# Shared accumulation banks in the up projection, both last down-projection pairs by seven products, and a denser weave in attention

## The chip, the cores and the metric

The kernel runs on one core of one Trainium2 chip. The metric is the device time of the execution in microseconds. A run's profile gives one execution: the time of each instruction on TensorE (PE), VectorE (DVE), ScalarE (ACT), GpSimd (POOL) and the DMA queues, which SyncE (SP), POOL and ACT issue.

## The reference

A decoder trunk of two layers over 256 tokens of width 2048, in fp32. Layer 0 has differential attention, layer 1 latent attention; each layer then attends to 256 memory tokens and ends in the MLP on which most of the change bears:

```
def sq_relu_mlp(h, wup, wdown):
    return jnp.square(jax.nn.relu(h @ wup)) @ wdown
...
        x = x + sq_relu_mlp(rms_norm(x, mlp_norm[i]), mlp_wup[i], mlp_wdown[i])
    return rms_norm(x, final_norm)
```

`wup` is 2048 x 8192, `wdown` 8192 x 2048. In layer 0, `x + o @ wo` closes the attention, with `wo` 2048 x 2048.

## The kernel before

**Precision.** A product of fp32 matrices is three matmuls: weight and activation are each split into a rounded half (hi) and a rest (lo), and hi x hi, hi x lo and lo x hi are summed in a PSUM bank. ScalarE makes a weight's hi (L211), VectorE its lo (L212), each in two pieces of 128x1024; four such pieces are kept, so a split is at most two items ahead of TensorE. Weights arrive in 1 MB tiles of 128x2048 (seven of them, the pool `wraw`).

**Items.** `fill` emits an item's load and split four items ahead of its matmuls. A plain *unit* is one weight tile against both halves of the tokens (t = 0, 1): 24 matmuls of 512 columns. A *product* is one weight tile against one half: 12 matmuls.

**Seven products.** A block of the MLP takes 1024 of the 8192 hidden columns, as two chunks of 512. Blocks 1 to 7 of the up projection (class `Seven`) compute the 2 x 2 blocks (two token halves, two weight columns) by seven products p1 to p7 instead of eight, each in two steps x = 0, 1, so 14 items where the plain way has 8 units. Sums of activations (forms s1 to s4) are made once, sums of weights per block: two by VectorE (L837, `add` in `job`), one by an accumulating DMA on POOL's queue (L829). Each product has its own PSUM bank; ScalarE copies p1 and p5 out (L905), VectorE adds and subtracts the others (L899), and `out` then applies ReLU and square (L1421, L1422), transposes on TensorE and splits the hidden block.

The down projection adds each block's part onto x in four column chunks c = 0 to 3: a chunk of a block has two units, `Chunk` joins the chunks of neighbouring blocks in one open pair of banks, and VectorE adds the closed sum to x (L515). Of the last block (7), columns 2 and 3 go by seven products (class `Final`, items Fp1 to Fp7), whose banks are added onto x by L1027; columns 0 and 1 are plain. `Final` shares banks already: p6 and p7 go onto p1's, p3 onto p5's. Its weight sums come from two accumulating DMAs (L949) and two additions of VectorE (L952).

**Order.** TensorE's order is written out. `mlp_line` merges the list `rest` (up units of block 0, down units) with the list `seven` so that VectorE's work, estimated by `vector`, and TensorE's, `tensor`, stay in step (`lead`); `late` holds back a down unit whose hidden block isn't ready. The merged list is the *line*. Before the change it ends with three down units (`after`) and then the *end*: 4 plain units and 7 products of `Final`. ScalarE's and VectorE's order is made by the framework's scheduler from the order of emission and estimated times. Transposes and the work behind them are side tasks: `pump`, called after every half item, emits those that an estimated clock calls due.

**Attention of layer 0.** The last two row groups of `wo` are added plainly (`project_group`). The first two go as two pairs (class `Pair`, columns 0-1 and 2-3) of seven products, one woven behind each of the 12 units of the last q, k, v projection and of the first two units of the next `project_group`. A pair's weight sums are four accumulating DMAs on POOL's queue (`onto`, L949). Meanwhile the last head group's softmax runs (L576 to L728), whose `a` (L728) TensorE then transposes (L168).

**Queues.** SP issues all weight loads in order, each waiting for a free tile; POOL issues the accumulating DMAs in order, each waiting for the split that last read its target and for the load before it.

Of the kernel before, what the change touches and what calls it, by code (L numbers as in the profile page):

```python
# [25 lines left out]
MLP_BLOCKS = 8  # L26
SEVEN = (1, 2, 3, 4, 5, 6, 7)
EVS = 7

# [18 lines left out]
def trunk(ctx, tc, x, xT, xT0, mem, memT, positions, gcols, gfinal, lam_vecs, consts, W, out):  # L48
# [214 lines left out]
    def matmul_chunk(acts, width=CH, turns=False, by_k=False):  # L263
# [11 lines left out]
        for u in range(n - 2 if turns else n):  # L275
            if weave:
                weave[0].step()
# [11 lines left out]
            if weave:  # L289
                weave.pop(0).emit()  # L290
# [500 lines left out]
    def plan_mlp(l):  # L791
        plan.extend(j for line in mlp_lines[l] for item in line for j in item.jobs)
# [21 lines left out]
    class Seven:  # L814
# [65 lines left out]
        def products(self, a, u, copied, out):  # L880
# [17 lines left out]
            def add(o, p, q, op=ALU.add):  # L898
                nc.vector.tensor_tensor(o, p, q, op)  # L899

            c = copied
            if p in ("p1", "p5", "p6", "p3"):
                c[p] = work.tile([P, CH], F32, tag="ev", name=nm(p), bufs=EVS)
            if p in ("p1", "p5"):
                nc.scalar.copy(c[p], o)  # L905
            elif p == "p6":
                add(c[p], o, c["p1"])
            elif p == "p3":
                add(c[p], o, c["p5"])
                add(c[p], c[p], c["p6"], ALU.subtract)  # L910
                out(0, 1, c[p], c[p])
            elif p == "p2":
                add(c["p1"], o, c["p1"])
# [9 lines left out]
    class Final:  # L923
# [3 lines left out]
        ORDER = "p1 p2 p5 p6 p3 p7 p4".split()  # L927

        def __init__(self, l):
            self.l, self.b = l, MLP_BLOCKS - 1  # L930
            self.cols = (2, 3)
# [3 lines left out]
            self.forms = {}  # L935

        def source(self, key):
            return W[f"mlp_wdown{self.l}"][8 * self.b + 2 * (1 + key % 10) + key // 10 - 1]

        def fetch(self, key):  # L940
            self.raw[key] = raw_tile()
            load(self.raw[key], self.source(key))

        def home(self, key):
            self.raw[key] = f32(unit()).rearrange("p a k t -> p (a k t)")
            return self.raw[key]

        def onto(self, o, key):
            tc.keep_in_program_order(nc.gpsimd.dma_start(self.raw[o], self.source(key), accum_op=ALU.add))  # L949

        def sum(self, o, a, b):
            nc.vector.tensor_tensor(self.home(o), self.raw[a], self.raw[b], ALU.add)  # L952

        def early(self):
            return [
                lambda hid: (
                    self.sums([k for c in range(2) for k in hid[self.b, c].tasks]),
                    self.fetch(11), load(self.home("t1"), self.source(11)),
                ),
                lambda hid: (self.onto("t1", 12), self.fetch(22), self.fetch(21)),  # L960
                lambda hid: (self.sum("t2", "t1", 22), self.sum("t4", "t2", 21)),
                lambda hid: self.fetch(12),
                lambda hid: self.onto(12, 22),
            ]

        def job(self, p):
            source = {"p1": 11, "p2": 21, "p3": 22, "p4": "t4", "p5": "t1", "p6": "t2", "p7": 12}[p]
            return lambda: halves_of(self.raw[source])

        def items(self):  # L970
            return [Item(self, p, [self.job(p)]) for p in self.ORDER]
# [27 lines left out]
        def products(self, inputs, p, nxt):  # L999
            where = Seven.A[p]  # L1000
            if p in ("p1", "p2", "p4"):
                t, c = where
                need(inputs[c].tasks)
# [17 lines left out]
            for t, j, op in {  # L1021
                "p1": ((0, 0, ALU.add),), "p5": ((1, 1, ALU.add),), "p6": ((0, 1, ALU.subtract),), "p3": ((0, 1, ALU.add),),
                "p7": ((1, 1, ALU.subtract), (1, 0, ALU.add)), "p2": ((0, 0, ALU.add),), "p4": ((1, 0, ALU.add),),
            }[p]:
                xc = xs[t][:, self.cols[j] * CH : (self.cols[j] + 1) * CH]
# [4 lines left out]
            done = {"p2": (2, 0), "p3": (3, 0), "p7": (3, 1), "p4": (2, 1)}  # L1030
            if nxt and p in done:
                nxt(*done[p], o)

    class Pair(Final):

        ORDER = "p1 p2 p5 p3 p6 p7 p4".split()
        FETCH = {"p1": ((11, 11), ("t", 12)), "p2": ((21, 21),), "p3": ((22, 22),)}
        STEP = {"p1": ("t", 11), "p5": ("t", 22), "p3": (22, 12), "p6": ("t", 21)}  # L1040
        SPLIT = {"p1": 11, "p2": 21, "p5": "t", "p3": 22, "p6": "t", "p7": 22, "p4": "t"}

        def __init__(self, name, first, cols, forms):
            self.name, self.first, self.cols, self.forms = name, first, cols, forms
            self.raw = {}
            self.banks = {}
            self.parts = {}
            self.steps = []
            self.splits = []

        def source(self, key):
            return W[self.name][4 * self.cols[key % 10 - 1] + self.first + key // 10 - 1]

        def part(self, t, c):
            if not self.parts:
                store = f32(unit()).rearrange("p a k (h t) -> p a (k h) t", t=P)
                self.parts = {(i, j): store[:, i, 4 * j : 4 * j + 4] for i in range(NT) for j in range(2)}
            return self.parts[t, c]

        def job(self, p):  # L1060
            def run():
                for key, at in self.FETCH.get(p, ()):
                    self.raw[key] = raw_tile()
                    load(self.raw[key], self.source(at))
                before = {"p5": ["p1"], "p6": ["p1", "p5"], "p7": ["p3"], "p4": ["p1", "p5", "p6"]}.get(p, [])
                assert all(i in self.steps for i in before)
                self.splits.append(p)
                return halves_of(self.raw[self.SPLIT[p]])

            return run  # L1070

        def items(self, inputs):
            return [Woven(self, p, inputs) for p in self.ORDER]

    class Woven:
# [3 lines left out]
        def step(self):  # L1079
            if self.p in self.of.STEP:  # L1080
                after = {"p5": "p5", "p3": "p3", "p6": "p6"}.get(self.p)
                assert after is None or after in self.of.splits
# [733 lines left out]
```

## Time and profile before

| what | value |
| --- | --- |
| runs shown, median | 2209.9 us (2209.76 to 2210.2, 3 runs) |
| the profiled execution | 2209.08 us |
| its span, first to last instruction | 2207.3 us |
| TensorE busy | 2191.9 us, 10511 matmuls |
| VectorE busy | 1814.2 us, 2025 instructions |
| ScalarE busy | 1388.1 us, 1855 instructions |
| granted TensorE clock, mean | 0.998 |
| DMA, mean | 213 GB/s |

The profiled execution is 1.8 us longer than its span, the time around the first and last instruction. A matmul's end is modelled, and matmuls overlap: one of 512 columns is shown as 0.39 us long, while the next starts about 0.227 us after it. In rows of instructions come start and length in us, engine, line, operation and what is written from what; brackets give idle time before it and who ended it. Tiles `pr` are banks of products, `mm` of plain units.

### The profile page before, as it was taken

What the parts mean: (1) busy time and instruction counts of PE and PEld (TensorE: products, weight loads), DVE (VectorE), ACT (ScalarE), POOL (GpSimd) and SP (SyncE); (2) the same over time, 40 slices, a digit from 0 to 9 for tenths busy, and PEclk for the clock granted to TensorE, in tenths of its full rate; (3) what the DMA queues carried; (4) which work ended last, traced back from release to release, by engine and by line L of the source; (5) the groups of instructions that cost most, each with busy time, mean ns of one, the idle gap of its engine ahead of it and who ended that gap; (6) DMA issues with size and microseconds to landing.
All of it is one profiled execution on the core that took longest, in us unless ns stands there. A gap on an engine that the chain in (4) does not pass through costs nothing.

```text
span 2207.3 us, 27663 instructions
## 1 busy us (share of the span) xinstructions
PE 2191.9 (99%) x10511; PEld 1838.4 (83%) x10511; DVE 1814.2 (82%) x2025; ACT 1388.1 (63%) x1855; POOL 147.6 (7%) x230
## 2 busy tenths in 40 slices
PE   9999999999999999999999999999999999999998
PEld 7888888888888888888889988888888888888886
DVE  6665878789889888889886878778988998898888
ACT  7555656666666666666665755656766666666665
POOL 1112210000000000000000411000000000000001
PEclk9999999999999999999999999999999999999999
DMA  9447796436766765865865344634767667677693
GB/s 384 156 155 250 221 268 252 153 124 203 266 204 207 263 203 217 254 214 210 273 213 191 133 155 155 246 134 153 225 232 228 209 249 224 199 258 221 203 297 105
DMA packets 71702, 469.43 MB, mean 213 GB/s; under 512 B 8208, under 2 KB 8592, under 8 KB 17808
## 3 DMA queue, kind: packets, MB, share of 16 engines
q1 hardware_dynamic: 65520, 425.19, 53.5%
q0 software_dynamic: 5760, 41.95, 10.3%
q8 instruction: 82, 1.34, 0.2%
q10 hardware_dynamic: 288, 0.52, 0.1%
q14 instruction: 52, 0.43, 0.1%
HBM read 465.53 MB, written 2.10 MB: 212 GB/s over the span
## 4 chain that ended last, share of the span: by engine, by line
PE 91%; DVE 5%; issue 1%; ACT 1%; DMA 1%; POOL 0%; SPq 0%; DVEq 0%; POOLq 0%; ACTq 0%
PE mm L164 61%; PE pr L164 25%; PE ax L164 2%; DVE wlo L212 2%; PE ax L168 2%; PE mm L168 1%; DVE raw L837 1%; ACT whi L211 1%; DVE unit L459 0%; DVE raw L487 0%; DMA raw<-in_mlp_wup_dram 0%; POOL rs L401 0%; DMA raw<-in_xT_dram 0%; DVE raw L470 0%; DVE x L515 0%
## 5 line engine op out<-in xcount | busy, mean ns | idle before, releaser
L211 ACT CAST whi<-raw 128x1024 fp32r<-128x1024 f32 (+2 forms) x974 | 1012.3, 1041 | 681.4 <-PE mm L164 520.1
L212 DVE TENSOR_TENSOR wlo<-raw,whi 128x1024 fp32r<-128x1024 f32 (+2 forms) x974 | 1161.3, 1210 | 287.7 <-ACT whi L211 272.0
L164 PE MATMUL mm<-whi,unit 128*128 128x512 f32 (+3 forms) x4160 | 1320.7, 389 | 0.6 <-ACT unit L389 0.6
L164 PEld LDWEIGHTS mm<-whi,unit 128*128 128x128 f32 x4160 | 778.0, 188 | 151.5 <-ACT unit L389 2.0
L164 PE MATMUL mm<-wlo,unit 128*128 128x512 f32 (+3 forms) x2080 | 802.8, 386 | 0.9 <-DVE wlo L212 0.8
L164 PE MATMUL pr<-whi,unit 128*128 128x512 f32 x1792 | 579.9, 392 | 0.0
L164 PEld LDWEIGHTS mm<-wlo,unit 128*128 128x128 f32 x2080 | 391.7, 188 | 74.0 <-DVE wlo L212 3.1
L164 PEld LDWEIGHTS pr<-whi,unit 128*128 128x128 f32 x1792 | 336.8, 188 | 69.2
L164 PE MATMUL pr<-wlo,unit 128*128 128x512 f32 x896 | 349.7, 390 | 0.6 <-DVE wlo L212 0.6
L837 DVE TENSOR_TENSOR raw<-raw,raw 128x2048 f32<-128x2048 f32 x84 | 192.3, 2289 | 28.7 <-DMA raw<-in_mlp_wup_dram 28.3
L164 PEld LDWEIGHTS pr<-wlo,unit 128*128 128x128 f32 x896 | 168.5, 188 | 36.0 <-DVE wlo L212 1.8
L829 POOL DMA_DIRECT2D raw<-in_mlp_wup_dram x28 | 24.6, 877 | 1094.8 <-DVE wlo L212 1094.8
L515 DVE TENSOR_TENSOR x<-x,mm 128x512 f32<-128x512 f32 x128 | 84.9, 682 | 3.6 <-PE mm L164 3.4
L401 POOL TENSOR_TENSOR rs<-rs,mhalf 128x1 f32<-128x1 f32 (+1 forms) x26 | 27.5, 1063 | 535.1 <-DVE rs L400 535.1
L356 ACT CAST unit<-ax 128x512 fp32r<-128x512 f32 x68 | 39.4, 582 | 25.7 <-PE ax L168 25.7
L899 DVE TENSOR_TENSOR p<-pr,p 128x512 f32<-128x512 f32 x70 | 47.9, 685 | 2.7 <-PE pr L164 2.7
L357 DVE TENSOR_TENSOR unit<-ax,unit 128x512 fp32r<-128x512 f32 x68 | 46.5, 686 | 1.5 <-ACT unit L356 1.1
L164 PE MATMUL mm<-unit,whi 128*128 128x256 f32 x256 | 47.1, 285 | 0.1
L168 PE MATMUL ax<-identr,p 128*128 128x128 f32 x304 | 46.2, 272 | 0.5 <-ACT unit L1650 0.5
L168 PEld LDWEIGHTS ax<-identr,p 128*128 128x128 f32 x304 | 37.6, 139 | 10.8 <-ACT unit L1650 0.9
L1421 ACT ACTIVATE p<-p,r 128x512 f32<-128x512 f32 x56 | 40.3, 720 | 9.6 <-DVE p L899 9.5
L164 PEld LDWEIGHTS mm<-unit,whi 128*128 128x128 f32 x256 | 40.0, 192 | 0.4 <-DVE unit L357 0.3
(185 smaller groups left out, 1147.0 us busy)
## 6 DMA issues: line engine op xcount, KB each, us to landing
raw<-in_mlp_wup_dram SPq DMA_DIRECT2D x128, 1024.0 KB, 4.9
raw<-in_mlp_wdown_dram SPq DMA_DIRECT2D x128, 1024.0 KB, 5.1
raw<-in_da_wqkv_dram SPq DMA_DIRECT2D x45, 1024.0 KB, 7.3
raw<-in_mlp_wup_dram POOLq DMA_DIRECT2D x28, 1024.0 KB, 8.2
raw<-in_da_wo_dram SPq DMA_DIRECT2D x16, 1024.0 KB, 6.8
raw<-in_ca_wkv_dram SPq DMA_DIRECT2D x16, 1024.0 KB, 5.0
raw<-in_mla_wo_dram SPq DMA_DIRECT2D x16, 1024.0 KB, 5.0
raw<-in_da_wo_dram POOLq DMA_DIRECT2D x8, 1024.0 KB, 10.6
```

The lines of the kernel that those rows point to most:

```text
L164: return nc.tensor.matmul(o, stationary, moving, start=start, stop=stop, skip_group_check=onto)
L168: nc.tensor.transpose(o, src, ident)
L211: nc.scalar.copy(hi, r)
L212: nc.vector.tensor_tensor(lo, r, f32(hi), ALU.subtract)
L356: nc.scalar.copy(hi, src)
L357: nc.vector.tensor_tensor(dst[:, 1, :n, t * P : (t + 1) * P], src, f32(hi), ALU.subtract)
L401: nc.gpsimd.tensor_tensor(r[:, :n], r[:, :n], mhalf.broadcast_to([P, n]), ALU.pow)
L515: nc.vector.tensor_tensor(xc, xc, ps, ALU.add)
L829: tc.keep_in_program_order(nc.gpsimd.dma_start(onto, src, accum_op=ALU.add))
L837: nc.vector.tensor_tensor(o, o, q, ALU.add)
L899: nc.vector.tensor_tensor(o, p, q, op)
L1421: nc.scalar.activation(r, src, AF.Relu, scale=rstd[t])
```

## The change

Three parts. **(1) Up products:** in `Seven`, p6, p7 and p4 accumulate onto the bank of p1 and p3 onto that of p5, so sums form in PSUM. ScalarE copies p1, p5 and p6 out; VectorE is left with one subtraction for p3, one addition for p2, one subtraction for p7; p4 goes from its bank straight into the ReLU. A rule `apart` keeps p4 from following its block's p7 directly while `rest` has an item. **(2) Down projection:** `Final` is gone. Both pairs of the last block are `Pair`s, A for columns 0-1 and B for 2-3, sharing activation sums; their weight sums are four accumulating DMAs each. Block 6's eight units and two of block 5 move behind the line and are interleaved with the 14 products in the order `CLOSING` (u is a unit). Steps, each a DMA on POOL's queue, are issued at the items given by `put`. **(3) Attention:** the 14 woven products go into the 12 units by `WEAVE`, up to two behind one unit; none is left for `project_group`.

```diff
+LAST = MLP_BLOCKS - 1
+WEAVE = "A1", "A2", "A5", "A3", "A6 B1", "A7 B2", "A4", "B5", "B3", "B6", "B7", "B4"
+CLOSING = "u A1 u A2 u B1 u A5 B2 u B5 A6 u A3 u B6 u B3 u A7 u A4 B7 B4"
...
         for u in range(n - 2 if turns else n):
-            if weave:
-                weave[0].step()
+            for item in weave[0] if weave else ():
+                item.step()
...
-            if weave:
-                weave.pop(0).emit()
+            for item in weave.pop(0) if weave else ():
+                item.emit()
...
-            if x == 0:
+            on = {"p6": "p1", "p7": "p1", "p4": "p1", "p3": "p5"}.get(p, p)
+            if x == 0 and on == p:
                 self.banks[p] = bank("pr")
-            o = self.banks[p]
+            o = self.banks[on]
...
-                    mmul(o, form[:, 0, kk], wh, kk == 0, False)
-                    mmul(o, form[:, 0, kk], wl, False, False)
-                    mmul(o, form[:, 1, kk], wh, False, kk == 7)
+                    mmul(o, form[:, 0, kk], wh, kk == 0 and on == p, False, on != p)
+                    mmul(o, form[:, 0, kk], wl, False, False, on != p)
+                    mmul(o, form[:, 1, kk], wh, False, kk == 7, on != p)
...
-            if p in ("p1", "p5"):
+            if p in ("p1", "p5", "p6"):
                 nc.scalar.copy(c[p], o)
-            elif p == "p6":
-                add(c[p], o, c["p1"])
             elif p == "p3":
-                add(c[p], o, c["p5"])
-                add(c[p], c[p], c["p6"], ALU.subtract)
-                out(0, 1, c[p], c[p])
+                nc.vector.tensor_tensor(c["p6"], o, c["p6"], ALU.subtract)
+                out(0, 1, c["p6"], c["p6"])
...
             elif p == "p7":
-                add(c["p6"], o, c["p6"])
-                add(c["p5"], c["p5"], c["p6"], ALU.subtract)
+                nc.vector.tensor_tensor(c["p5"], c["p5"], o, ALU.subtract)
                 out(1, 1, c["p5"], c["p5"])
             else:
-                add(c["p6"], o, c["p6"])
-                out(1, 0, c["p6"], c["p6"])
+                out(1, 0, o, c["p4"])
...
+    class Pair:
+        FETCH = {"p1": (11, "t"), "p2": (21,), "p3": (22,)}
+        STEP = {"p1": ("t", 11), "p5": ("t", 22), "p3": (22, 12), "p6": ("t", 21)}
+        SPLIT = {"p1": 11, "p2": 21, "p5": "t", "p3": 22, "p6": "t", "p7": 22, "p4": "t"}
...
+        def step(self, p):
+            o, key = self.STEP[p]
+            assert p == "p1" or p in self.splits
             tc.keep_in_program_order(nc.gpsimd.dma_start(self.raw[o], self.source(key), accum_op=ALU.add))
+            self.steps.append(p)
...
-            chunks += [Chunk(l, "down", groups[i], c, close=False) for c in pairs[1]]
+            chunks += [Chunk(l, "down", groups[i], c, close=False) for c in pairs[1] if i < LAST - 2 or c == 2]
...
-        rest = up(0, 1) + [i for b in range(MLP_BLOCKS - 1) for i in down(b)]
+        rest = up(0, 1) + [i for b in range(LAST - 1) for i in down(b)]
...
-        rest, after = rest[:-3], rest[-3:]
...
-            late = rest and of.kind == "down" and any(usable.get(h, math.inf) > now for h in of.halves)
-            take_seven = seven and (not rest or late or lead <= 0)
+            late = rest and of.kind == "down" and usable.get(of.halves[rest[0].u], math.inf) > now
+            apart = seven and seven[0].u == ("p4", 0) and line[-1].of is seven[0].of
+            take_seven = seven and (not rest or late or (lead <= 0 and not apart))
...
-        end = down(len(groups) - 1)
-        for item, step in zip(after + end, end[-1].of.early()):
-            item.early = step
-        return line + after, end
+        plain = [
+            i
+            for c in range(4)
+            for i in Chunk(l, "down", both(LAST - 2, *both(LAST - 1)) if c == 3 else both(LAST - 1), c, open=c != 2).items()
+        ]
+        forms = {}
+        pairs = {k: Pair(f"mlp_wdown{l}", 8 * LAST, 2, c, forms) for k, c in (("A", (0, 1)), ("B", (2, 3)))}
+        end = []
+        at = {}
+        for word in CLOSING.split():
+            at[word] = len(end)
+            if word == "u":
+                end.append(plain.pop(0))
+            else:
+                of, p = pairs[word[0]], "p" + word[1]
+                end.append(Item(of, p, [of.job(p)]))
...
+        put(0, lambda hid: pairs["A"].sums([k for c in range(2) for k in hid[LAST, c].tasks]))
+        for k, of in pairs.items():
+            put(max(0, at[k + "1"] - 3), lambda hid, of=of: of.fetch("t", of.home()))
+            put(at[k + "1"] - 1, lambda hid, of=of: of.step("p1"))
+        for p in ("p5", "p6", "p3"):
+            for k, of in pairs.items():
+                put(at[k + p[1]] - 3, lambda hid, of=of, p=p: of.step(p))
+        for i, todo in steps.items():
+            end[i].early = lambda hid, todo=todo: [do(hid) for do in todo]
+        return line, end, pairs["A"]
```

More of the change, by code (lines that the diff above doesn't have):

```diff
@@ L934, in __init__ @@
             self.parts = {}
-            self.forms = {}
+            self.steps = []
+            self.splits = []
         def source(self, key):
[L938 to L946, printed above, removed]
@@ L966, in job, with fetch @@
-        def job(self, p):
[L967 to L971, printed above, removed]
+            at = 12 if key == "t" else key
+            return W[self.name][self.first + self.stride * self.cols[at % 10 - 1] + at // 10 - 1]
+        def fetch(self, key, home=None):
+            if key not in self.raw:
+                self.raw[key] = raw_tile() if home is None else home
+                load(self.raw[key], self.source(key))
@@ new lines, in home, with run @@
+        def home(self):
+            return f32(unit()).rearrange("p a k t -> p (a k t)")
+        def step(self, p):
+            o, key = self.STEP[p]
+            assert p == "p1" or p in self.splits
+            tc.keep_in_program_order(nc.gpsimd.dma_start(self.raw[o], self.source(key), accum_op=ALU.add))
+            self.steps.append(p)
+        def job(self, p):
+            def run():
+                for key in self.FETCH.get(p, ()):
+                    self.fetch(key)
+                before = {"p5": ["p1"], "p6": ["p1", "p5"], "p7": ["p3"], "p4": ["p1", "p5", "p6"]}.get(p, [])
+                assert all(i in self.steps for i in before)
+                self.splits.append(p)
+                return halves_of(self.raw[self.SPLIT[p]])
+            return run
@@ L973, in keep, with part @@
+        def part(self, t, c):
+            if not self.parts:
+                store = f32(unit()).rearrange("p a k (h t) -> p a (k h) t", t=P)
+                self.parts = {(i, j): store[:, i, 4 * j : 4 * j + 4] for i in range(NT) for j in range(2)}
+            return self.parts[t, c]
         def keep(self, t, c, src):
@@ L1029, in products @@
                     added.append(summed)
[L1030 to L1073, printed above, removed]
+                if landed:
+                    landed(c, t, o, p in ("p2", "p3", "p7", "p4"))
     class Woven:
@@ L1165, in trunk @@
+    plan += [("da_wo", 4 * c + 2, CH) for c in range(4)]
     plan_k("ca_wkv0", 4)
@@ L1459, in run @@
                     continue
[L1460 to L1461 removed]
+                if isinstance(of, Pair):
+                    of.products([hid[LAST, c] for c in range(2)], item.u, landed)
                     continue
@@ L1473, in run @@
                 if item.u == n - 1 and of.close:
-                    finish_chunk(of, sums.pop((of.kind, of.c)), nxt)
-        line, end = mlp_lines[l]
+                    finish_chunk(of, sums.pop((of.kind, of.c)), landed)
+        line, end, pair = mlp_lines[l]
         limit = free_banks[0] - 1
```

117 lines of the change are left out of this document (50 added, 67 removed).

## The prediction

> **What bounds the kernel now.** I read the page first, then TensorE's waits, then the chain of waits.
>
> ```profile
> span 2207.3 us, 27663 instructions
> ...
> PE 2191.9 (99%) x10511; PEld 1838.4 (83%) x10511; DVE 1814.2 (82%) x2025; ACT 1388.1 (63%) x1855; POOL 147.6 (7%) x230
> ...
> PE 91%; DVE 5%; issue 1%; ACT 1%; DMA 1%; POOL 0%; SPq 0%; DVEq 0%; POOLq 0%; ACTq 0%
> ```
>
> The first line is the span, the second each engine's busy share, the third the shares of the chain that ended last. TensorE is busy for all but 2207.3 - 2191.9 = 15.4 us, most of it before the first and after the last matmul. VectorE, at 82%, is second.
>
> ```profile
> PE ax L168 <- DVE a L728: 1.2, 1, 1.2
> PE mm L164 <- DVE wlo L212: 0.8, 2, 0.4
> PE pr L168 <- DVE x L1027: 0.6, 1, 0.6
> PE pr L164 <- DVE wlo L212: 0.6, 2, 0.3
> ```
>
> These are the waits of TensorE that the change can reach (total us, times, longest). They come to 3.2 us. So the kernel can gain by fewer matmuls and hardly by anything else, and every wait that the change puts in front of TensorE is paid in full.
>
> ```profile
> 537.72 5.44 PE mm L164 x24
> 543.16 5.44 PE pr L164 x24
> ```
>
> Start, length, count, from the chain: 24 matmuls of 512 columns take 5.44 us, plain (mm) or of seven products (pr): 0.2267 us each. A plain unit (24 matmuls) is 5.44 us, a product (12) 2.72 us.
>
> **a. The second pair by seven products.** Of the last block's down projection, columns 2 and 3 go by seven products already. Columns 0 and 1 take 4 plain units, 4 x 24 = 96 matmuls a layer. They become 7 x 12 = 84. Two layers: 24 matmuls less, 24 x 0.2267 = **-5.4 us**. That block 6's units and one chunk of block 5 move behind the line changes no count. Attention keeps all its products.
>
> **b. The shared banks.** p6, p7 and p4 now add onto the bank of p1, p3 onto that of p5. A product's first matmul must wait until the bank's last reader is through. I worked out the order of items by the planner's rule. p1 to p6, p5 to p3 and p6 to p7 always have at least a product and a unit between them, 8.2 us, and p7 to p4 has one unit, 5.44 us, since `apart` holds p4 back. At one place it can't: `rest` is used up when block 7's last product comes, and each layer's line ends "unit, p7, p4, p4". There p4 waits for VectorE's subtraction (now `c5 - o`) from that bank. What it will take is seen at the same product of before:
>
> ```profile
> 2127.75 0.39 PE L164 MATMUL pr<-whi,unit 128*128 128x512 f32 x1
> 2127.98 0.39 PE L164 MATMUL mm<-whi,unit 128*128 128x512 f32 x1
> ```
>
> ```profile
> 2126.55 2.58 DVE L212 TENSOR_TENSOR wlo<-raw,whi 128x1024 fp32r<-128x1024 f32 x2
> 2129.05 0.69 DVE L899 TENSOR_TENSOR p<-pr,p 128x512 f32<-128x512 f32 x1
> ```
>
> The product's last matmul starts at 2127.75, and the next item, which today needs nothing, at 2127.98. VectorE is splitting weights until 2129.1 and reads the bank until 2129.74. TensorE starts about 0.05 us after such an end (below). So p4 starts at about 2129.79: 1.8 us late, twice: **+3.6 us**. From below: with VectorE free, the read would start at the matmul's end, 2127.75 + 0.39 = 2128.14, and p4 at 2128.88: 0.9 us, +1.8 in all. From above, the slowest kind of such read in the line:
>
> ```profile
> 1710.95 5.46 PE mm L164 x24
> ```
>
> ```profile
> 1714.32 0.68 DVE L899 TENSOR_TENSOR p<-pr,p 128x512 f32<-128x512 f32 x1
> ```
>
> The unit behind p7 starts at 1710.95 and the read ends at 1715.00: 4.1 us with the restart, +8.2 in all. I take 1.8, from the very place; no next block's sums crowd VectorE there. At the other p7s the same 4.1 us stay under the unit's 5.44 us, so they cost nothing, and would cost the excess if the read came 1.4 us later.
>
> The new sharing also moves work: per block VectorE loses four of seven additions (p6's, p4's, and one each of p3's and p7's two), ScalarE gains p6's copy.
>
> ```profile
> L899 DVE TENSOR_TENSOR p<-pr,p 128x512 f32<-128x512 f32 x70 | 47.9, 685 | 2.7 <-PE pr L164 2.7
> L905 ACT COPY p<-pr 128x512 f32<-128x512 f32 x28 | 16.2, 577 | 0.0
> L899 DVE TENSOR_TENSOR p<-p,p 128x512 f32<-128x512 f32 x28 | 19.2, 686 | 0.0
> ```
>
> Of 98 additions 42 are left (3 in each of 14 blocks); 56 x 0.685 = 38 us of VectorE's time go. Hidden behind TensorE, that is worth only the waits that it shortens.
>
> **c. Attention packed.** The 14 woven products go into 12 units instead of 14, so two products no longer stand beside the last group's softmax.
>
> ```profile
> 348.61 0.39 PE L164 MATMUL mm<-whi,unit 128*128 128x512 f32 x1
> 350.16 0.44 PE L168 MATMUL ax<-identr,a 128*128 128x128 f32 x2 [1.16 <-DVE a L728]
> ```
>
> ```profile
> 349.64 0.47 DVE L728 SCALAR_TENSOR_TENSOR a<-p,rsum,a 128x256 f32<-128x256 f32 x1
> ```
>
> TensorE restarts 0.05 us after VectorE's end at 350.11. In this stretch VectorE is full:
>
> ```profile
> 270.00:280.00 10.00, 10.00 (x50) 8.36 (x49) 6.95 (x9) 5.56 (x7) 0.87 (x1) 1.00 1.00 268
> 280.00:290.00 10.00, 10.00 (x46) 8.29 (x45) 7.65 (x8) 4.99 (x5) 0.00 (x0) 1.00 1.02 382
> ...
> 330.00:340.00 10.00, 10.00 (x53) 8.53 (x53) 9.97 (x17) 6.03 (x15) 0.00 (x0) 1.00 0.71 253
> 340.00:350.00 10.00, 9.00 (x43) 7.14 (x41) 9.86 (x19) 6.60 (x15) 0.00 (x0) 1.00 0.35 123
> ```
>
> After the stretch come its length and the busy us of TensorE, weight loads, VectorE, ScalarE and POOL, then the granted clock, the DMA share and GB/s. Each product moved away takes two splits (2 x 1.2) and one or two additions with it, some 6 us from the 20 that are full, so most of the 1.2 us wait should go: **-1.0**. It goes where VectorE has room (7.0 and 7.7 of 10) but DMA has none (1.00 and 1.02). TensorE loses nothing there now; bounds: -1.2 from the wait row, and +1.2 if the crowding only changes its place.
>
> **d. Waits at the start of the line.** The 0.8 us row above (one wait per layer) is at the first unit behind "p4 p4 p1 p1 p5", five products running. p4's addition goes from that run, so I take **-0.7** of the 0.8 (bounds -0.8 and 0). The wait of pr for wlo, 0.6 us, comes earlier, where nothing is lighter yet, and stays.
>
> **e. Block 7's run.** There six products run together, "p4 p4 p1 p1 p5 p5", with one more sum of 2.29 us inside.
>
> ```profile
> 2061.03 2.36 DVE L212 TENSOR_TENSOR wlo<-raw,whi 128x1024 fp32r<-128x1024 f32 x2 [0.31 <-ACT whi L211]
> 2063.30 2.29 DVE L837 TENSOR_TENSOR raw<-raw,raw 128x2048 f32<-128x2048 f32 x1
> ```
>
> ```profile
> 2064.45 0.39 PE L164 MATMUL mm<-whi,unit 128*128 128x512 f32 x1
> ```
>
> Today's run of five ends at 2064.45 with the next split done at 2063.39, 1.1 us in hand. The sum takes 2.3 from that, two additions fewer give 1.3 back, so it stays at about zero: **+0.3** (bounds 0 and 2 x 1.1).
>
> **f. The closing.** Now 10 units and 14 products: 54.4 + 38.1 = 92.5 us a layer. Its transfers are 18 loads and 8 accumulating ones:
>
> ```profile
> q1 hardware_dynamic: 65520, 425.19, 53.5%
> q0 software_dynamic: 5760, 41.95, 10.3%
> ```
>
> 425.19 MB are 405 MB-sized loads (1.049 MB) in 53.5% of the span: 2.91 us of all 16 engines each. The accumulating ones, 40 in 10.3%: 5.68 us each. So 18 x 2.91 + 8 x 5.68 = 97.8 us of transfers in 92.5. That fits only because loads run ahead:
>
> ```profile
> 1092.89 0.42 SPq L183 DMA_DIRECT2D unit<-in_mlp_wdown_dram  x1
> ```
>
> ```profile
> 1106.01 10.93 PE mm L164 x48
> ```
>
> Today's first transfer for the closing leaves 13 us before the line's end, and its SP queue holds weights of units behind it. The tightest link is t += 22 between A5 and A6 on the POOL queue: it waits for A5's split. POOL's later steps queue behind it, and A6's split, with what stands behind that on ScalarE and VectorE, waits for its landing.
>
> ```profile
> DMA to landing us min/median/max: 8.0/10.8/13.6
> ```
>
> A5 starts 4 x 5.44 + 3 x 2.72 = 29.9 us into the closing, A6 another 3 x 2.72 + 5.44 later, at 43.5. How far a split runs ahead shows at today's p5:
>
> ```profile
> 2173.76 3.45 DVE L212 TENSOR_TENSOR wlo<-unit,whi 128x1024 fp32r<-128x1024 f32 x2
> ```
>
> ```profile
> 2178.56 2.72 PE pr L164 x12
> ```
>
> It ends at 2177.21, some 1.2 us before its product. So A5's ends at 28.7, t lands at 39.5 (36.7 to 42.3), and A6 wants its split begun 2.3 us ahead, at 41.2. So the median is 1.7 us early, the slowest 1.1 late: **+0.4** for two layers (bounds 0 and 2.2). [...]
>
> VectorE in the closing: the last 91.6 us of today's matmuls hold about as many splits.
>
> ```profile
> 2106.00:2197.60 91.60, 91.60 (x412) 75.50 (x410) 78.07 (x83) 57.90 (x74) 6.23 (x5) 1.00 0.58 195
> ```
>
> 78.1 us busy; 2 more splits of a whole weight (+4.7) and some 8 additions onto x (+5), less two sums of 2.29 us, gives some 83 of 92.5: it fits. Column 0 ends only two products before the next layer's first unit. I take that as nothing: today's wait there (0.6 us, for p7's addition onto x) has an easier run before it.
>
> **Sum.** -5.4 + 3.6 - 1.0 - 0.7 + 0.3 + 0.4 = -2.8 us. The profiled execution took 2209.08 us, its span 2207.3 and 1.8 around it; the median of the runs is 2209.9, 0.8 above it. From the median: **2207.1 us**.
>
> **Rivals.**
> R1, the waits are cheaper: p4 waits 0.9 us only, c and d go whole (-1.2, -0.8), e and f are 0. -5.4 + 1.8 - 2.0 = -5.6: 2204.3 us. For it speaks that nothing else is queued on VectorE with urgency; against it the row at 2129.05.
> R2, the closing becomes bound by transfers: 97.8 - 92.5 = 5.3 us a layer, 10.6 in all in place of f: 2207.1 - 0.4 + 10.6 = 2217.3 us, slower. It decides once the closing's transfers lead its matmuls by less than 5.3 us. The 13 us at 1092.89 speak against it, and so do the 20 us from 270 to 290, with full transfers and TensorE busy throughout; that an accumulating transfer can't leave before a split speaks for it.
> R3, p4's read falls behind a crowd: 4.1 us twice, 2207.1 - 3.6 + 8.2 = 2211.7 us. The rows of 1710 to 1715 speak for it, block 7's own row against it.
> R4, R3 with TensorE slow after each such wait. The kernel's first matmuls, after idleness, ran so:
>
> ```profile
> 1.23 4.02 PE L1216 MATMUL ax<-blank 128*128 128x512 bf16 x9 [1.23 <-DVE coef L1298]
> ```
>
> Nine in 4.02 us, 0.447 each instead of 0.2267. Another 4.02 us at that rate lose 9 x 0.22 = 2.0 us at each of the two places: 2215.7 us, slower. No wait inside this kernel is over 1.2 us and the clock column stays at 1.00, so no row shows that a wait brings it. [...]
> That the change doesn't do what it says, no matmul fewer, the count of items rules out.
>
> **How the numbers follow.** A measurement of this kernel can tell about 0.2%, 4.4 us: faster is under 2205.5, slower over 2214.3. The forecast gets 0.46, R1 0.30, R2 0.14, R3 0.07, R4 0.03. So faster is 0.30, same 0.46 + 0.07 = 0.53, slower 0.14 + 0.03 = 0.17. The range takes in R1, with 0.7 us for waits that I didn't see go, and R3, with 1.8 us for a lead in the closing that falls short in part; R2 and R4 in full stay out: 2203.6 to 2213.5.
>
> **What would show it.** a: 24 fewer matmuls of 512 columns, still 0.2267 us each. b: two waits of TensorE "pr" for VectorE's subtraction, near 1.8 us each, and none elsewhere in the line. c: the wait for L728 gone, no new one between 240 and 330 us. d: the wait near 610 us gone. f: no wait of ScalarE or TensorE on mlp_wdown beyond 1 us. The forecast is wrong if p4 doesn't wait (another engine order), if the closing's DMA share sits at 1.0 with waits behind it, or if waits grow inside blocks 2 to 6.

## The result, and the profile after the change

The changed kernel takes 2213.89 us (median of 22 runs, 2211.41 to 2216.61), the kernel before 2210.55 us (22 runs, 2208.87 to 2213.59) on the same chips: ratio 1.0016, 95% interval 1.0009 to 1.0022. The change costs 3.3 us where I forecast a gain of 2.8. The direction was wrong, and the time lies above my range.

The page of the changed kernel, the three lines that answer to those of before:

```profile
span 2214.8 us, 27687 instructions
...
PE 2191.8 (99%) x10487; PEld 1836.2 (83%) x10487; DVE 1798.2 (81%) x1991; ACT 1408.7 (64%) x1879; POOL 155.8 (7%) x242
...
PE 89%; DVE 5%; DMA 2%; issue 1%; ACT 1%; POOL 1%; DVEq 0%; POOLq 0%; ACTq 0%
```

There are 24 matmuls fewer, and TensorE is "busy" as long as before: busy time hides matmuls that run slowly (below, from 1172 to 1178 us, 20 matmuls are shown as 5.98 us of it). The waits of TensorE (total us, times, longest) show more:

```profile
PE pr L167 <- DVE p L914: 3.5, 2, 1.7
PE mm L167 <- DVE unit L360: 2.9, 1, 2.9
PE mm L167 <- DVE wlo L215: 2.7, 2, 1.7
PE pr L167 <- DVE wlo L215: 1.6, 4, 0.5
```

(Lines stand 3 further down than before: L164 is now L167, L212 is L215, L357 is L360; the addition onto x is L1026.) The first row is the wait that I forecast. The second and the third are new and not in my sum.

To place all of it I added up, from both traces, by how much the starts of neighbouring matmuls lie further apart than usual for their size (0.227 us for 512 columns, 0.173 for 384, 0.109 for 128). That is TensorE's loss: 13.5 us before, 26.9 after. How small excesses are counted moves both totals and hardly their difference: with only those above 0.1 us they are 11.2 and 25.1.

| place | before | after | difference |
| --- | --- | --- | --- |
| first 13 us | 1.3 | 2.1 | +0.8 |
| attention, transposes at 351 us | 1.4 | 1.0 | -0.4 |
| start of the line, 610 and 1645 us | 1.3 | 0 | -1.3 |
| block 2, 647 and 1688 us | 0.3 | 3.2 | +2.8 |
| block 7's run, 1005 and 2046 us | 0 | 0.8 | +0.8 |
| p4 behind p7, 1062 and 2103 us | 0 | 3.8 | +3.8 |
| change of layer, 1162 to 1178 us | 1.1 | 6.1 | +5.0 |
| closing of layer 1, A6 at 2155 us | 0 | 0.8 | +0.8 |
| closing of layer 1, last split, 2204 us | 0 | 0.8 | +0.8 |

That is +13.1 of the +13.4; the other places agree. The first row is chance: the profiles of the experiments, none of which touches it, have 0.4 to 2.2 us there. With -5.4 for 24 matmuls and -1.0 for a shorter end (9.0 us instead of 10.1 from the last matmul's start to the last instruction) it comes to 6.7 of the 7.5 us between the two spans; the rest is spread thin. The profiled execution (2216.61 us) is the slowest of its kernel, the one of before (2209.08) among the fastest, so a part of the 7.5 us is chance of an execution. Which part, the experiments show.

The change of layer, in the changed kernel's timeline:

```profile
1160.68 0.69 DVE L1026 TENSOR_TENSOR x<-x,pr 128x512 f32<-128x512 f32 x1
...
1163.68 0.60 PE L171 MATMUL pr<-identr,x 128*128 128x128 f32 x4
...
1166.89 0.68 DVE L365 TENSOR_TENSOR xg<-pr,g 128x512 f32<-128x512 f32 x1
...
1167.68 0.51 PE L167 MATMUL mm<-whi,unit 128*128 128x384 f32 x2
...
1167.84 0.62 ACT L359 CAST unit<-xg 128x512 fp32r<-128x512 f32 x1
...
1168.79 0.34 PE L167 MATMUL mm<-wlo,unit 128*128 128x384 f32 x1
...
1171.29 0.68 DVE L360 TENSOR_TENSOR unit<-xg,unit 128x512 fp32r<-128x512 f32 x1
...
1172.02 1.01 PE L167 MATMUL mm<-whi,unit 128*128 128x384 f32 x2 [2.89 <-DVE unit L360]
```

A4's addition onto column 0 ends at 1161.37. Then come the transposes, the gain (L365), the rounded half (L359) and the rest (L360), each behind other work of its engine. ScalarE has the rounded half at 1168.46, but VectorE has three splits, B4's addition and another column's gain ahead, and the rest is there at 1171.97. TensorE waits 2.9 us, and two matmuls of 384 columns then take 1.01 us where two of them took 0.51 at 1167.68. The view by windows says why:

```profile
1172.00:1178.00 6.00, 5.98 (x20) 5.88 (x21) 2.50 (x6) 0.83 (x1) 0.55 (x1) 0.51 0.34 116
```

The granted clock, the first column behind POOL's, is 0.51: from 1172.0 to 1177.9 us TensorE runs at half speed and loses 2.8 us more.

### The profile page after: what moved, and what is told of

It reads as the page before. It is cut to its first block, busy times and chain, and to the rows that moved or that the text cites. A ratio compares the mean times of both kernels' runs of the same rounds, so it can differ in the third digit from the quotient of the medians.

```text
span 2214.8 us, 27687 instructions
## 1 busy us (share of the span) xinstructions
PE 2191.8 (99%) x10487; PEld 1836.2 (83%) x10487; DVE 1798.2 (81%) x1991; ACT 1408.7 (64%) x1879; POOL 155.8 (7%) x242
## 4 chain that ended last, share of the span: by engine, by line
PE 89%; DVE 5%; DMA 2%; issue 1%; ACT 1%; POOL 1%; DVEq 0%; POOLq 0%; ACTq 0%
PE mm L167 58%; PE pr L167 26%; DVE wlo L215 3%; PE ax L167 2%; PE ax L171 2%; DMA raw<-in_mlp_wdown_dram 1%; PE mm L171 1%; DMA raw<-in_mlp_wup_dram 1%; ACT whi L214 1%; DVE raw L840 1%; DVE unit L462 0%; DVE raw L490 0%; POOL rs L404 0%; DVE x L518 0%; DVE raw L473 0%
## 5 line engine op out<-in xcount | busy, mean ns | idle before, releaser
L214 ACT CAST whi<-raw 128x1024 fp32r<-128x1024 f32 (+3 forms) x998 | 1038.5, 1042 | 669.8 <-PE mm L167 518.0
L215 DVE TENSOR_TENSOR wlo<-raw,whi 128x1024 fp32r<-128x1024 f32 (+3 forms) x998 | 1192.6, 1211 | 333.1 <-ACT whi L214 307.5
L167 PE MATMUL mm<-whi,unit 128*128 128x512 f32 (+3 forms) x4032 | 1282.4, 389 | 3.8 <-DVE unit L360 2.9
L167 PEld LDWEIGHTS mm<-whi,unit 128*128 128x128 f32 x4032 | 755.6, 188 | 150.7 <-DVE unit L360 3.2
L167 PE MATMUL mm<-wlo,unit 128*128 128x512 f32 (+3 forms) x2016 | 777.8, 386 | 2.7 <-DVE wlo L215 2.7
L167 PE MATMUL pr<-whi,unit 128*128 128x512 f32 x1904 | 618.0, 392 | 3.5 <-DVE p L914 3.5
L167 PEld LDWEIGHTS mm<-wlo,unit 128*128 128x128 f32 x2016 | 380.4, 189 | 73.4 <-DVE wlo L215 4.1
L167 PEld LDWEIGHTS pr<-whi,unit 128*128 128x128 f32 x1904 | 357.4, 188 | 77.8 <-ACT whi L214 4.3
L167 PE MATMUL pr<-wlo,unit 128*128 128x512 f32 x952 | 371.3, 390 | 1.9 <-DVE wlo L215 1.6
L167 PEld LDWEIGHTS pr<-wlo,unit 128*128 128x128 f32 x952 | 178.8, 188 | 40.5 <-DVE wlo L215 4.4
L840 DVE TENSOR_TENSOR raw<-raw,raw 128x2048 f32<-128x2048 f32 x84 | 191.9, 2285 | 17.0 <-DMA raw<-in_mlp_wup_dram 16.6
L359 ACT CAST unit<-ax 128x512 fp32r<-128x512 f32 x66 | 38.2, 582 | 20.9 <-PE ax L171 20.9
L167 PE MATMUL mm<-unit,whi 128*128 128x256 f32 x256 | 47.1, 285 | 0.1
L360 DVE TENSOR_TENSOR unit<-ax,unit 128x512 fp32r<-128x512 f32 x66 | 44.9, 682 | 0.1
L167 PEld LDWEIGHTS mm<-unit,whi 128*128 128x128 f32 x256 | 39.9, 191 | 0.3 <-DVE unit L360 0.3
L398 ACT ACTIVATE junk<-x 128x512 bf16<-128x512 f32 x56 | 35.1, 627 | 7.4 <-DVE x L1026 5.7
```

The source lines that it names most:

```text
L167: return nc.tensor.matmul(o, stationary, moving, start=start, stop=stop, skip_group_check=onto)
L214: nc.scalar.copy(hi, r)
L215: nc.vector.tensor_tensor(lo, r, f32(hi), ALU.subtract)
L359: nc.scalar.copy(hi, src)
L360: nc.vector.tensor_tensor(dst[:, 1, :n, t * P : (t + 1) * P], src, f32(hi), ALU.subtract)
L398: return nc.scalar.activation(junk[:, : src.shape[1]], src, AF.Square, scale=scale, accum_out=acc)
```

## The experiments

All times stand beside runs of the kernel before on the same chip. The changed kernel was run again beside the next three experiments; the others ran on two other chips, where the ratio to before is the fairer measure. T is my theory after the comparison: three separate waits, made by the order of the items, and a clock that falls behind the longest.

### The changed kernel again

> The changed kernel, unaltered, once more. Its profiled execution lost 26.9 us of TensorE's time beyond the usual distance of its matmuls' starts, the kernel before 13.5. If that list is a property of the kernel, the same places come back: 6.1 us at the change of layer (3.3 of waiting and 2.8 of matmuls at a granted clock of 0.51), 1.9 us twice where p4 follows p7, 1.85 and 1.3 us in block 2 of the two layers; a time of 2213 to 2217 us, ratio 1.0009 to 1.0022 to the kernel before. If some of it is chance of one execution, it is the slow matmuls of the first 10 us (2.1 against 1.3 us) and the slow stretch at 1172 us.

2213.82 us (11 runs), ratio 1.0014 (1.0005 to 1.0023). TensorE's loss was 26.5 us, at the same places and of the same size within 0.5 us, the change of layer included (3.3 of waiting, 2.9 of slow matmuls). The list belongs to the kernel.

### Column 1 first

```diff
-    LATE = (0, 1, 3, 2)
+    LATE = (1, 0, 3, 2)
```

> The changed kernel with one tuple altered: the next layer's first projections take column 1 of x ahead of column 0 (LATE = 1, 0, 3, 2). Theory T: column 0, finished only by A4, two products before the layer's end, makes TensorE wait 2.9 us for VectorE's L360, and that idleness halves its clock for 5.5 us more; column 1 is through 8.2 us earlier, so the wait, and the slow stretch with it, goes: 6.1 us at the change of layer fall to 1 or less, time 2213.9 - 5 = 2208.9 us. Rival U: all four columns now end late and VectorE is simply full there, so that the wait moves to the second or third unit: 2212 to 2214 us, waits of 2 us or more for L360 or wlo between 1165 and 1185.

2208.98 us, 4.8 less than the changed kernel's 2213.82; ratio to the kernel before 0.9993 (0.9984 to 1.0002). The same stretch, from its view by windows:

```profile
1172.00:1178.00 6.00, 6.00 (x36) 6.00 (x35) 5.09 (x10) 2.86 (x5) 1.73 (x1) 1.00 0.61 208
```

36 matmuls instead of 20 in 6 us, at a clock of 1.00. No wait for L360 is left, and TensorE loses nothing from 1160 to 1220 us. So the wait didn't move on (rival U): it came from the choice of the column that is finished last but two products.

### A unit between p7 and p4

```diff
+        line[-4], line[-3] = line[-3], line[-4]
```

> The changed kernel with two neighbours of each layer's line swapped, so that its end reads p7, unit, p4, p4 in place of unit, p7, p4, p4. If p4 only waits for VectorE's read of the shared bank, both waits of 1.9 us go and nothing comes: -3.8, 2210.1 us. If the three products p7, p2, p7 now running together outrun their splits, 1 to 2 us come back as waits for wlo: 2211 to 2213 us.

First the place in the changed kernel, TensorE and then VectorE:

```profile
1062.42 0.39 PE L167 MATMUL pr<-whi,unit 128*128 128x512 f32 x1
1064.54 0.47 PE L167 MATMUL pr<-whi,unit 128*128 128x512 f32 x1 [1.74 <-DVE p L914]
```

```profile
1061.21 2.59 DVE L215 TENSOR_TENSOR wlo<-raw,whi 128x1024 fp32r<-128x1024 f32 x2 [1.31 <-ACT whi L214]
1063.71 0.68 DVE L914 TENSOR_TENSOR p<-p,pr 128x512 f32<-128x512 f32 x1
```

p7's last matmul starts at 1062.42, its bank is read only when two splits are through, until 1064.39, and p4 starts 1.9 us late. With the unit between, the row of L914 is gone from the waits, nothing came at the run p7, p2, p7, and the time is 2209.99 us: 3.8 us less, as expected; ratio to before 0.9997 (0.9988 to 1.0005).

### One swap in block 2

In block 2 the line has p6, p3, unit where blocks 3 and 4 have p6, unit, p3:

```diff
+        for i in range(1, len(line)):
+            a, b, c = line[i - 1 : i + 2] if i + 1 < len(line) else (None,) * 3
+            if a and [x.u for x in (a, b)] == [("p6", 1), ("p3", 1)] and getattr(c.of, "kind", "") == "down":
+                line[i], line[i + 1] = c, b
```

> The changed kernel with one swap in block 2 of each layer: p6, unit, p3 in place of p6, p3, unit, as blocks 3 and 4 have it. At that place VectorE sits idle 4.2 us before a sum of weights (L840) whose load came late, with the split that TensorE waits for behind it in its queue; TensorE waits 1.85 us in layer 0 and 1.3 us in layer 1. If the order of the items is the cause (the load gets its tile later than before), both go: -3 us, 2211 us. If the merging that places sums ahead of splits is to blame whatever the order, a wait for wlo of 1 us or more stays between 640 and 660 us and the time is 2213 to 2214 us.

The place in the changed kernel: SP's queue, then the timeline.

```profile
622.84 0.33 SPq L186 DMA_DIRECT2D raw<-in_mlp_wdown_dram  x1
636.44 0.33 SPq L186 DMA_DIRECT2D raw<-in_mlp_wup_dram  x1
```

```profile
646.10 2.29 DVE L840 TENSOR_TENSOR raw<-raw,raw 128x2048 f32<-128x2048 f32 x1 [4.21 <-DMA raw<-in_mlp_wup_dram]
...
648.30 4.62 DVE L215 TENSOR_TENSOR wlo<-raw,whi 128x1024 fp32r<-128x1024 f32 x4
...
649.58 0.50 PE L167 MATMUL mm<-wlo,unit 128*128 128x512 f32 x1 [1.69 <-DVE wlo L215]
```

SP holds the load of p2's second weight from 623.2 to 636.4, until a split frees a tile. It lands at 646.1. The sum that needs it serves a product at 655.4, yet it stands in VectorE's queue ahead of the split that a unit needs at 647.7. VectorE idles 4.2 us, then sums, then splits. With the swap SP issues the load at 632.41, 4.0 us earlier, and VectorE sums at 637.74 without idling. Both waits are gone, and VectorE's idle time before its sums, over the kernel, falls from 16.6 to 9.0 us. The time is 2211.95 us, 1.9 less than the changed kernel and not the 3 expected; the trace lost 3 us less at the two places, and a median of executions that lie between 2209.15 and 2213.97 can't tell 1.9 from 3.

This run gave something else. Its wait for L360 at the change of layer was the same 2.90 us, and no matmul was slow:

```profile
1168.60:1174.60 6.00, 5.90 (x35) 5.86 (x36) 3.97 (x9) 2.46 (x4) 0.55 (x1) 1.00 0.34 117
```

In the run with the unit between, the same wait was followed by a part of it, 1.7 us:

```profile
1167.80:1173.80 6.00, 6.00 (x27) 5.90 (x28) 3.04 (x6) 2.08 (x3) 0.55 (x1) 0.72 0.35 118
```

The same 2.9 us of idleness cost nothing, 1.7 or 2.8 to 2.9 us. That is the chance part, and the traces show what it goes with. In the changed kernel's trace the granted clock changes at 1171.06, 1177.88 and 2208.71 us, 2 and then 302 steps of 3.413 us; with the unit between it is at 0.50 for one such step. Cut at these steps, the windows of the changed kernel read:

```profile
1167.65:1171.06 3.41, 1.48 (x8) 0.87 (x6) 3.41 (x5) 1.88 (x5) 0.00 (x0) 1.00 0.45 142
1171.06:1174.47 3.41, 2.45 (x8) 2.45 (x9) 1.79 (x6) 0.93 (x2) 0.55 (x1) 0.50 0.78 284
1174.47:1177.88 3.41, 3.41 (x14) 3.31 (x13) 1.65 (x2) 0.07 (x1) 0.00 (x0) 0.50 0.05 19
```

those of the run with the unit between:

```profile
1164.72:1168.13 3.41, 0.52 (x3) 0.36 (x3) 3.41 (x7) 1.23 (x3) 0.00 (x0) 1.00 0.78 234
1168.13:1171.54 3.41, 3.41 (x14) 3.31 (x13) 1.42 (x4) 0.83 (x1) 0.55 (x1) 0.50 0.55 192
```

and those of the swap, whose clock doesn't fall here (steps counted back from its fall at 2201.50, behind the last matmul):

```profile
1163.85:1167.26 3.41, 1.96 (x11) 1.34 (x9) 3.41 (x6) 1.87 (x5) 0.00 (x0) 1.00 0.55 151
1167.26:1170.67 3.41, 1.97 (x11) 1.93 (x12) 2.35 (x7) 1.48 (x4) 0.55 (x1) 1.00 0.84 305
```

The first time behind the length is TensorE's busy time. Where one step holds 1.93 or 2.89 us of the wait (busy 1.48 or 0.52), the next ran at 0.50. In the changed kernel, busy for 2.45 us in that one, a second followed; with the unit between, busy for 3.41, none did. Where the wait is cut in the middle, 1.45 and 1.44 us, the clock stayed at 1.00. So in these traces the loss goes with where the wait lies among the steps. All steps at full clock in the traces of the changed kernel (from 10.52 us, where its clock's record begins) and the kernel before (from 5.72) sort alike: the one with 1.93 us of idleness and those at the two kernels' ends (2.50 us from 2205.30, before: 2.86 from 2197.08) have a step at 0.50 behind them, and none with 1.74 us or less has. That is read from traces; no run shifts the wait on purpose.

### TensorE kept busy through the wait

```diff
                 for t in range(NT):
+                    if filler and u == h == 0 and t == 1:
+                        o = bank("pr")
+                        for _ in range(filler):
+                            nc.tensor.matmul(o, acts[0].get(0, 0, 0), hi[:, :CH], start=True, stop=True)
                     part(u, h, hi, lo, t)
...
+    ps = matmul_chunk(acts, LAT, filler=14)
```

> The changed kernel with 14 more matmuls of 512 columns into a spare bank, which nothing reads, between the two halves of the next layer's first unit, so that TensorE is busy (14 x 0.227 = 3.2 us) through the wait of 2.9 us. The wait for column 0 itself stays. Theory T: the slow matmuls behind the wait are TensorE's clock falling after idleness; with the filler the granted clock stays at 1.00 from 1167 to 1180 us and what that stretch lost by slowness (2.8, 2.9, 1.7 and 0 us in four executions so far, 1.9 on average) goes: about -1.6 us, 2212.2 us, and the executions lie closer together than the 5.7 us of the changed kernel. Rival V: the slow stretch comes from something else that happens there (late weights, transfers of the next layer): it stays, 2213.9 us or, with the filler behind the wait, more.

2212.60 us, 1.2 less than the changed kernel (on another chip) though 14 matmuls are added; ratio to before 1.0008 (0.9999 to 1.0017); 11 runs within 3.4 us. The stretch that holds the filler and what follows:

```profile
1167.00:1173.00 6.00, 6.00 (x33) 5.25 (x32) 4.96 (x11) 2.07 (x4) 0.55 (x1) 1.00 0.72 242
```

The clock stays at 1.00 there and in the 5 us behind. One profiled execution alone could be the chance seen in block 2's run, and the median can't decide: its interval overlaps the changed kernel's (1.0005 to 1.0023). Nor can the spread: with the unit between, where the wait stays, 11 runs lie within 2.4 us. But each execution's mean granted clock is on record. The profiled executions that lost 2.8 us or more have 0.997, the one that lost 1.7 has 0.998, and those without a slow stretch 0.998 or 0.999. Of the changed kernel's 33 executions 9 have 0.997 (median 2215.4 us), 19 have 0.998 (2213.7) and 5 have 0.999 (2212.3). With the filler none of 11 has 0.997 and 7 have 0.999; with column 1 first, alone and in the later kernels, none of 26 has 0.997 and 21 have 0.999. So in these runs idleness is what brings the slow stretch (T); rival V, late weights or transfers, would have kept it.

### The three alterations together, and a fourth

> The changed kernel with the three alterations together: column 1 first, the unit between p7 and p4, the swap in block 2. By themselves they gave 4.8, 3.8 and 1.9 us. If they are separate waits they add up: 2213.9 - 10.5 = 2203.4 us, ratio to the kernel before 0.9965, TensorE's loss beyond the usual distances some 14 us or less (kernel before: 13.5), and what is left of the gain is the 5.4 us of the 24 matmuls and 1.7 us of the waits that the change took away at the start of the line and in attention. If VectorE is what holds all three, less comes: 2206 to 2208 us with new waits for wlo.

2203.12 us, ratio to before 0.9963 (0.9950 to 0.9975): 10.7 us below the changed kernel (10.6 when each is set against the kernel before on its chip) where 10.5 were expected. The waits add up. TensorE's loss is 13.8 us, the kernel before's 13.5; one wait behind a late load (1.4 us at 540) came in this execution.

The fourth alteration is in the closing:

```diff
-CLOSING = "u A1 u A2 u B1 u A5 B2 u B5 A6 u A3 u B6 u B3 u A7 u A4 B7 B4"
+CLOSING = "u A1 u A2 u B1 u A5 B2 u B5 u A6 A3 u B6 u B3 u A7 u A4 B7 B4"
```

> The kernel of the three alterations with one more in the order of the closing: A6 one unit later (B5 u A6 A3 in place of B5 A6 u A3). In layer 1 of the changed kernel ScalarE waits 5.5 us for the accumulating transfer between A5 and A6, and TensorE 0.8 us at A6. If that link is the cause the 0.7 us go and nothing comes: 2202.7 us. If the next steps of the queue are only pushed on, a wait of 0.5 us or more appears at A3, B6 or A7: 2203.4 us or more.

The place in the changed kernel, POOL's queue and then ScalarE's:

```profile
2132.95 3.61 POOL L1690 TENSOR_TENSOR x<-x,unit 128x512 f32<-128x512 f32 x1 [34.53 <-DMA raw<-in_mlp_wdown_dram]
2136.50 0.88 POOL L954 DMA_DIRECT2D raw<-in_mlp_wdown_dram  x1
2141.52 0.88 POOL L954 DMA_DIRECT2D raw<-in_mlp_wdown_dram  x1 [4.13 <-DVE wlo L215]
```

```profile
2153.99 3.90 ACT L214 CAST whi<-raw 128x1024 fp32r<-128x1024 f32 x4 [5.47 <-DMA raw<-in_mlp_wdown_dram]
```

The step between A5 and A6 leaves at 2141.52 and ScalarE starts A6's split at 2153.99, 12.5 us later; A6 is due at 2155.43. One unit later the loss at A6 is gone and nothing came at the next steps: 2201.10 us, ratio to before 0.9955 (0.9943 to 0.9968). Of the 2.0 us below the three alterations 0.8 are this wait; the rest is within what the medians scatter.

### Attention spread again

```diff
-WEAVE = "A1", "A2", "A5", "A3", "A6 B1", "A7 B2", "A4", "B5", "B3", "B6", "B7", "B4"
+WEAVE = "A1 A2 A5 A3 A6 A7 A4 B1 B2 B5 B3 B6 B7 B4".split()
```

The last two entries stand behind units of `project_group` again, and the plan of loads follows.

> The changed kernel with attention's 14 products spread again, one behind each of 14 units, as before the change. If packing them is what shortened the wait before the row group's transposes (1.4 us before, 1.0 after), it is 1.4 us again between 345 and 355 us, and nothing else in that part differs: 0.4 us, less than one time can show. If packing cost time anywhere in attention, TensorE loses less between 200 and 350 us than in the changed kernel, which loses nothing there above 0.2 us.

One execution: TensorE loses 1.4 us at 349 us, as the kernel before, where the packed order loses 1.0, and nothing else in attention differs. So packing was worth 0.4 us. The 2.8 us of slow matmuls at the change of layer came again.

### The last split

```diff
-    weighted = {(0, 0): nc.gpsimd, (1, 0): nc.gpsimd, (0, 1): nc.vector, (1, 1): nc.vector}
+    weighted = {(0, 0): nc.gpsimd, (1, 0): nc.vector, (0, 1): nc.vector, (1, 1): nc.gpsimd}
```

> The kernel of the four alterations with one more at the very end: the multiplication of x by the final gain for token half 1 of column 0 goes from GpSimd to VectorE, and that of column 1 from VectorE to GpSimd. In the changed kernel GpSimd's (1.29 us) starts with the last product's split on VectorE, which takes 2.33 us in place of 1.22, and TensorE loses 0.8 us at 2204; in the run with column 1 first, which loses nothing there, GpSimd's takes 2.41 and the split 1.22. Theory: the two engines shut each other out; with column 1's piece (ready some 9 us earlier) on GpSimd the last split is 1.22 again and the 0.8 us go: 2200.4 us against 2201.1, less than this comparison can show, so the rows decide. Rival: VectorE is simply full there and the 0.7 us of its new piece delay the split as much: the 0.8 us stay.

GpSimd and VectorE at the end of the changed kernel:

```profile
2202.35 1.29 POOL L1690 TENSOR_TENSOR x<-x,unit 128x512 f32<-128x512 f32 x1 [2.00 <-ACT junk L398]
```

```profile
2202.39 2.33 DVE L215 TENSOR_TENSOR wlo<-raw,whi 128x1024 fp32r<-128x1024 f32 x1
```

and of the kernel with the engines exchanged, VectorE alone:

```profile
2187.68 1.22 DVE L215 TENSOR_TENSOR wlo<-raw,whi 128x1024 fp32r<-128x1024 f32 x1
2188.81 0.68 DVE L1695 TENSOR_TENSOR x<-x,unit 128x512 f32<-128x512 f32 x1
```

The last split is 1.22 us long again, VectorE's new piece stands behind it, and TensorE loses nothing there: the rows decide for the theory. 2200.42 us, ratio to before 0.9953 (0.9939 to 0.9966). This version beats both kernels: 10.9 us under the kernel before on its chip (2211.32). The two profiled spans differ by 7.9 us (2207.3 and 2199.4): 5.4 are the matmuls, 1.8 the smaller loss of TensorE (11.7 us), 1.0 the shorter end. Together that is 0.3 too much, which shows how exact such a count is. The kernel before's profiled execution is one of its fast ones, so the medians differ by more.

## Why the prediction was wrong, step by step

- **a, 24 matmuls: right.** 10511 became 10487.
- **b, p4 behind p7: right.** 1.9 us twice, 3.8 against 3.6 forecast, for the reason given (two splits ahead of the read), and 3.8 came back with the unit between. No other p7 made p4 wait, so R3 (4.1 us each) didn't come either.
- **c, attention: right in sign, too large.** -0.4 against -1.0. I counted the splits that leave the full stretch, but one still stands directly ahead of the `a` (now L731) that TensorE waits for:

```profile
350.59 1.22 DVE L215 TENSOR_TENSOR wlo<-raw,whi 128x1024 fp32r<-128x1024 f32 x1
351.72 0.61 DVE L731 SCALAR_TENSOR_TENSOR a<-p,rsum,a 128x128 f32<-128x128 f32 x2
```

- **d, start of the line: right, larger.** Both waits went whole: -1.3 against -0.7.
- **e, block 7's run: +0.8 against +0.3**, inside its bounds.
- **f, the A5 to A6 link: +0.8 against +0.4**, in layer 1 alone. The place and the link were right. The transfer took 12.5 us until ScalarE could start. R2, transfers as the bound, didn't come: from 1067 to 1169 us, with the first closing, the DMA share is 0.87, from 2108 to 2207, with the second, 0.76.
- **f, column 0: this step failed.** "Column 0 ends only two products before the next layer's first unit. I take that as nothing". It cost 5.0 us of the profiled execution and, as its removal showed, 4.8 of the median: the largest part of the 6.1 us between my -2.8 and the measured +3.3. I had seen the place and the two products, 5.4 us, and not worked out the chain behind them: addition, transposes, gain, cast, subtraction, 11.3 us here from 1160.68 to 1171.97, on engines with full queues. "An easier run before it" was an argument about TensorE's wait of before, which had another cause.
- **R4, the clock: it fell behind a wait, but at another place.** I let it follow p4's waits and gave it 0.03. In the changed kernel's trace the step of each p4 wait holds 1.74 us of idleness, and the clock stayed at 1.00 behind it; the 2.9 us at the change of layer brought 0.50 there, with 1.93 us in one step, and with the unit between, with 2.89. In block 2's run, with 1.45 and 1.44 in two steps, it stayed at 1.00.
- **Block 2: not in the sum at all**, 2.8 us in the profile. I named it only as what would prove me wrong ("if waits grow inside blocks 2 to 6"). I had worked out the new order of items and used it for shared banks, not for where the loads get their tiles.
- **The last split (+0.8) and the shorter end (-1.0)** weren't seen and cancel.

My own terms came to -1.7 instead of -2.8, an error of 1.1 us. What I didn't price cost 5.0 + 2.8 + 0.8 - 1.0 = 7.6 us in the profile. With the two omitted waits and p4's removed, the change is worth 7.8 us (2203.12 against 2210.95): the idea was sound, and the order of its items took the gain away. None of the alterations was run in the kernel before; at the change of layer it loses 1.1 us, a part of which column 1 first might win there too.

## What to carry to other kernels

When items are reordered, work out for each consumer behind the new order the whole chain from its last producer, engine by engine with what is queued there, and not the number of items between. In block 2 an early sum that waited for a late load (VectorE idle for 4.2 us) held up the split queued behind it, and TensorE waited 1.7 us for that: look where a load gets its tile. A wait of TensorE of 2.9 us is priced with a slow stretch behind it, which cost between nothing and the same again here (0, 1.7 and 2.8 to 2.9 us).

## What the runs showed of the hardware

- Behind the 2.9 us of waiting at the change of layer the granted clock was 0.50 for two steps of 3.41 us (changed kernel) or one (unit between), or stayed at 1.00 (block 2's run), by where the wait lay among these steps. In the traces of the changed kernel and the kernel before, the least idleness in one step with 0.50 behind it is 1.93 us, the most without it 1.74. The slow matmuls cost up to 2.9 us.
- VectorE's last split and GpSimd's product with the final gain hardly overlapped: started 0.04 us apart, either the split took 2.33 us and the product 1.29 (changed kernel), or 1.22 and 2.41, so the one held up ended 1.1 us behind the other. The second case is from the run with column 1 first:

```profile
2195.43 2.41 POOL L1690 TENSOR_TENSOR x<-x,unit 128x512 f32<-128x512 f32 x1 [2.00 <-ACT junk L398]
```

```profile
2195.47 1.22 DVE L215 TENSOR_TENSOR wlo<-raw,whi 128x1024 fp32r<-128x1024 f32 x1
```

In both cases GpSimd's record starts first, so the records don't tell beforehand who wins.
